# Six modulation products and the branch for large counts change places around the expert loop of a two-layer transformer

## The chip, the cores and the metric

The kernel runs on one core of one Trainium2 chip. The metric is the device time of one execution in microseconds (us), the median of several runs. A profile is one execution recorded by the hardware. The engines have short names in it: PE is TensorE's matrix multiplications and PEld its weight loads, DVE is VectorE, ACT is ScalarE, POOL is GpSimd, SP is SyncE, which only issues transfers here. A "q" behind a name means the engine's sequencer or its queue of transfers.

## The reference

Two layers work on 256 latent and 256 context tokens of 1024 features. Each layer derives six modulation vectors from a condition, mixes the tokens, and sends them through a mixture of experts (top 2 of 16). Cut to that:

```
mod   = silu(c)     @ w_ada[l] + b_ada[l]      # 6 * 1024: sh1, sc1, g1, sh2, sc2, g2
mod_c = silu(c_ctx) @ w_ada[l] + b_ada[l]
u = layer_norm(h) * (1 + sc1) + sh1
m = mixer(u)            # layer 0: window attention beside a gated recurrence; layer 1: gated linear attention, FFT
h = layer_norm_affine(alpha * h + g1 * m)
u = layer_norm(h) * (1 + sc2) + sh2
probs = softmax(u @ w_router);  two experts per token, weights w
y = sum_e gates[e] * ((silu(u @ w1[e]) * (u @ w3[e])) @ w2[e])
h = layer_norm_affine(alpha * h + g2 * y)
```

## The kernel before

The program is written with a tile framework: a scheduler orders each engine's instructions by program order and readiness, and sets the semaphores. An `If` block is a unit for it; on every engine that takes part it becomes a register load, a compare and a branch, and, where the block is skipped, events that make up for its semaphores.

**Modulation products.** The 6144 columns of `w_ada` are done in twelve products per layer, j = 0 to 11, of 512 columns. `ada_load` brings 2 MB in two loads on SP's queue into tiles "w" of the pool `wp` (three buffers). `ada_part` (L248) does eight fp32 matmuls with a 32-column stationary tile in four column groups. `ada_col` (L260) turns the result into columns: a ScalarE copy, four small matmuls (L265) and a VectorE addition. `ada_row` (L271) makes rows of it: bias on VectorE, then a broadcast matmul (L281) and a ScalarE copy (L282) for each of two destinations. j = 10 and 11 of layer 0 are the vector g2, which scales the expert output; j = 0 to 3 of layer 1 are the shift and scale that layer 1 uses first.

**Layer 0's mixer** (`mixer0`, L631) does four products at its start. The others come from a generator `fill0` (L656): one step of it is taken ahead of each of twelve weight slices of the input projections, and the remaining steps between the first steps of the recurrence (`hgrn`) and ahead of the attention. The projections are fp32r matmuls in three passes (L372).

**Router** (L499). It ranks the tokens of each expert and writes, by a matmul of one-hot matrices (L597 to L599), a list of token rows: tile `io`, with 64 rows for each of 8 units per expert. The counts go to `cni`.

**Experts of layer 0** (`moe0`, L1492). Token rows `u_d` lie in HBM. For each of 16 experts POOL gathers 64 rows, and 64 more if the count asks for it (`gathers`, L1568), by indirect transfers; TensorE transposes them (L1548), multiplies with the gate and up weights (L1478) and the down weights (L1485); ScalarE and VectorE copy the result out (L1559), and POOL scatters it to `y_d` (L1538). A third unit has its own gather. Weights come by SP's queue in tiles of 1 MB through a ring of 14 slots (`Ring`, `load_more`, L1448): nine of a pool `wx`, two of "m", three of `wp`. An expert's loads wait until a slot's last user is done. More than three units per expert are handled by `large()` (L1642), a block that stands behind the loop and is skipped when no expert has so many.

**Layer 1's mixer** (`mixer1`, L1083) loads the expert output back (`y_load`, L1119, four transfers on SP's queue), weighs the two rows of a token (L1130, L1131), scales by g2 (L1133), and normalises twice (`block`) before TensorE transposes the tokens (L1148). Two such blocks, b = 2 and 3, run interleaved, and the first weight slice of layer 1 is loaded and split into two fp32r parts (`cols_w`, L1099; ScalarE L353, VectorE L355).

## Time and profile before

| | us |
|---|---|
| median of 3 runs | 1477.45 |
| lowest and highest | 1475.44, 1483.96 |
| the profiled execution | 1482.15 |
| its span in the profile | 1480.1 |
| TensorE busy in the span | 1243.6 (84%) |
| VectorE, ScalarE, POOL busy | 603.8, 353.3, 101.0 |
| mean granted TensorE clock | 0.914 of full speed |
| HBM traffic | 303 MB read, 211 GB/s over the span |

How to read it: the busy share is a mean over stages. The stages of layer 0 are the projections (to 256 us), recurrence and attention (to 430), output projection and router (to 517), experts (525 to 848). Layer 1's mixer follows from there to about 1157, and its experts to 1460. What an edit is worth depends on the stage: on who is full there, and on what the others wait for. The clock is a share of 2.4 GHz; 0.50 is 1.2 GHz.

### The profile page before, as it was taken

The numbers are of one execution on the slowest core, as the hardware profiler recorded it, in microseconds if no ns is written. First come the engines' busy times: TensorE is split into PE (matmuls) and PEld (weight loads), VectorE is DVE, ScalarE is ACT, GpSimd is POOL, SyncE is SP. The second block draws the span as 40 slices with busy tenths as digits, with TensorE's granted clock in tenths as the row PEclk, the third lists the DMA queues.
The fourth block names the chain that finished last, engine by engine and source line by source line (L and its number), as shares of the span: only waits on it lengthen the run. The fifth ranks groups of instructions, "written<-read, shape, count | busy, mean of one in ns | idle before, by whom it ended". The sixth has DMA issues, their size and how long they took to land. (4 is left out here: it accounts for less than half of the span.)

```text
span 1480.1 us, 19008 instructions
## 1 busy us (share of the span) xinstructions
PE 1243.6 (84%) x7269; PEld 746.9 (50%) x7269; DVE 603.8 (41%) x1408; ACT 353.3 (24%) x691; POOL 101.0 (7%) x134
## 2 busy tenths in 40 slices
PE   4899999988879479999999806999977788988883
PEld 2677888455659433333333305888537443434331
DVE  5332422575857811212212148736558232222123
ACT  2333223354543110111111113442222110101001
POOL 1000000110011120211100000000010000000000
PEclk9899999897969689999999956999998899999896
DMA  8465574610012599999978052322284799988631
GB/s 296 154 231 182 185 242 173 200 29 1 1 30 86 208 328 379 362 361 380 357 280 313 14 165 82 116 64 90 86 307 144 294 394 393 383 320 324 238 134 59
DMA packets 152225, 310.32 MB, mean 210 GB/s; under 512 B 7596, under 2 KB 39660, under 8 KB 152088
## 3 DMA queue, kind: packets, MB, share of 16 engines
q1 hardware_dynamic: 146320, 296.44, 56.9%
q0 software_dynamic: 4608, 8.59, 2.0%
q10 hardware_dynamic: 1160, 3.48, 0.6%
q8 instruction: 84, 1.38, 0.4%
q14 instruction: 53, 0.43, 0.1%
HBM read 303.24 MB, written 9.44 MB: 211 GB/s over the span
## 5 line engine op out<-in xcount | busy, mean ns | idle before, releaser
L372 PE MATMUL mm<-wh,uT 128*128 128x256 f32 (+2 forms) x960 | 193.6, 297 | 7.8 <-ACT uT L353 4.8
L372 PEld LDWEIGHTS mm<-wh,uT 128*128 128x128 f32 x960 | 158.9, 198 | 21.0 <-issue 8.2
L372 PE MATMUL mm<-wl,uT 128*128 128x256 f32 (+2 forms) x480 | 141.6, 296 | 4.2 <-DVE wl L355 4.0
L1478 PE MATMUL mm<-wx,xT 128*64 128x512 f32 x504 | 143.3, 600 | 1.6 <-PEq L1619 0.8
L372 PEld LDWEIGHTS mm<-wl,uT 128*128 128x128 f32 x480 | 94.9, 198 | 6.0 <-DVE wl L355 5.4
L355 DVE TENSOR_TENSOR wl<-w,wh 128x2048 fp32r<-128x2048 f32 (+3 forms) x33 | 53.8, 1646 | 70.6 <-ACT wh L353 52.9
L1478 PEld LDWEIGHTS mm<-wx,xT 128*64 128x64 f32 x504 | 44.5, 137 | 66.6 <-issue 64.8
L1463 DVE TENSOR_TENSOR hs<-hs,mm 64x512 f32<-64x512 f32 x32 | 22.1, 691 | 127.7 <-ACT hs L1462 81.6
L254 PE MATMUL mm<-w,sT 128*32 128x512 f32 x384 | 61.7, 646 | 10.0 <-DMA w<-in_w_ada_dram 10.0
L372 PE MATMUL mm<-uT,wh 128*128 128x512 f32 (+1 forms) x208 | 59.9, 375 | 4.9 <-ACT wh L353 4.9
L1478 PE MATMUL ac<-wx,xT 128*64 128x512 f32 x216 | 60.3, 595 | 3.7 <-PEq L1865 2.1
L353 ACT CAST wh<-w 128x2048 fp32r<-128x2048 f32 (+3 forms) x33 | 45.8, 1388 | 67.2 <-DMA w<-in_w_in_even_dram 53.0
L372 PE MATMUL mm<-wo,mx 128*128 128x256 f32 x384 | 51.5, 292 | 6.3 <-ACT wo L353 3.5
L1478 PE MATMUL tr<-wx,xT 128*64 128x512 f32 x200 | 51.9, 620 | 5.1 <-PEq L1865 2.1
L1485 PE MATMUL mm<-wx,hT 128*64 128x512 f32 x192 | 54.1, 597 | 1.7 <-PEq L1634 1.0
L1462 ACT ACTIVATE hs<-mm 64x512 f32<-64x512 f32 x32 | 18.9, 590 | 147.2 <-PE mm L1478 94.4
L372 PEld LDWEIGHTS mm<-wo,mx 128*128 128x128 f32 x384 | 48.6, 197 | 7.1 <-ACT wo L353 3.8
L1478 PE MATMUL mm<-w,xT 128*64 128x512 f32 x120 | 47.0, 596 | 0.3 <-PEq L1621 0.2
L372 PEld LDWEIGHTS mm<-uT,wh 128*128 128x128 f32 (+1 forms) x208 | 37.0, 188 | 14.3 <-ACT wh L353 5.2
L1559 DVE COPY ys<-mm 64x512 f32<-64x512 f32 x22 | 15.3, 693 | 67.6 <-ACT ys L1559 64.4
L1478 PE MATMUL ac<-w,xT 128*64 128x512 f32 x88 | 41.5, 626 | 1.4 <-DMA wx<-in_w_expert_up_dram 0.7
L1148 PE MATMUL tr<-cst,yk 128*128 128x128 f32 x32 | 5.6, 334 | 43.2 <-ACT yk L1141 43.2
(472 smaller groups left out, 2162.6 us busy)
## 6 DMA issues: line engine op xcount, KB each, us to landing
w<-in_w_ada_dram SPq DMA_DIRECT2D x48, 1024.0 KB, 5.4
wx<-in_w_expert_up_dram SPq DMA_DIRECT2D x45, 1024.0 KB, 8.5
wx<-in_w_expert_gate_dram SPq DMA_DIRECT2D x42, 1024.0 KB, 7.9
wx<-in_w_expert_down_dram SPq DMA_DIRECT2D x42, 1024.0 KB, 8.0
w<-in_w_in_even_dram SPq DMA_DIRECT2D x13, 1024.0 KB, 10.1
w<-in_w_expert_down_dram SPq DMA_DIRECT2D x13, 1024.0 KB, 7.6
w<-in_w_expert_gate_dram SPq DMA_DIRECT2D x12, 1024.0 KB, 8.8
w<-in_w_expert_up_dram SPq DMA_DIRECT2D x12, 1024.0 KB
```

What stands on the lines that cost most here:

```text
L254: nc.tensor.matmul(ps[32 * g:32 * g + 32, :], sT[:, k, :], ws[k // 4][:, k % 4, :], start=k < 4, stop=k >= 4, skip_group_check=True, tile_ ...
L353: nc.scalar.copy(hi, src)
L355: nc.vector.tensor_tensor(lo, src, hi.bitcast(FP), op=OP.subtract)
L372: nc.tensor.matmul(ps, lhs(i, k), rhs(j, k), start=(k == 0 and n == 0), stop=(k == nk - 1 and n == 2))
L1148: nc.tensor.transpose(ps[:, k * 128:(k + 1) * 128], y[:, kk_ * 128:(kk_ + 1) * 128], ident)
L1462: nc.scalar.activation(hs, hp[0:64, :], AF.Silu)
L1463: nc.vector.tensor_tensor(hs, hs, hp[64:128, :], op=OP.mult)
L1478: nc.tensor.matmul(hp[i * 64:i * 64 + 64, :], xT(k), ws[2 * i + k // 4][:, k % 4, :], start=k == 0, stop=k == 7, skip_group_check=True, ti ...
L1485: nc.tensor.matmul(yp[n * 64:n * 64 + 64, :], hT[:, k, :], ws[4 + k // 2][:, k % 2, n * 512:(n + 1) * 512], start=k == 0, stop=k == 3, ski ...
L1559: (nc.vector.tensor_copy if n else nc.scalar.copy)(ys[:, ns], yp[rs_, :])
```

## The change

The products j = 10, 11 of layer 0 and j = 0 to 3 of layer 1 leave `fill0` and stand behind the last expert. Their weights are loaded through the expert ring, and the first weight slice of layer 1 (`pre`) through `wp`. `large()` stands ahead of the first expert, behind the first two gathers, and takes the slots that are free then. The index list `io` has 128 rows, so that a gather or scatter moves up to 128 rows in one transfer, without a second one and its branch; the one-hot tiles are fp32 instead of fp32r for that. The row loads of b = 2 and 3 go out on POOL's queue. The splits of `pre` stand ahead of the blocks b = 2 and 3, whose VectorE and ScalarE instructions are held in program order. In the ring the three slots of `wp` now come ahead of the two of "m".

```diff
@@ modulation products
+    def ada_load(l, j, ring=None):
         src = w_ada[l][:, j * 512:(j + 1) * 512]
-        return [load_w(src[q * 512:(q + 1) * 512, :], 4, 512) for q in range(2)], (l, j)
+        ws = []
+        for q in range(2):
+            w = ring.tile([128, 4, 512]) if ring else wp.tile([128, 4, 512], FP, name="w", tag="w")
+            nc.sync.dma_start(w, src[q * 512:(q + 1) * 512, :].rearrange("(k p) n -> p k n", p=128))
+            ws.append(w)
+        return ws, (l, j)
...
+    def ada_row(l, j, dsts, add1=0.0, col=False, ld=None, bz_=None):
+        ld = ld or ada_load(l, j)
+        if bz_ is None:
+            bz_ = bz
+            nc.gpsimd.dma_start(bz[0:2, :], b_ada[l:l + 1, j * 512:(j + 1) * 512].to_broadcast([2, 512]))
...
@@ router
-                self.io = cp.tile([64, 2, 16 * NU], I32, name="io")
+                self.io = cp.tile([128, 2, 8 * NU], I32, name="io")
...
-            R = self.p.tile([128, 2, 64], FP if self.l else FR, name="rR", bufs=1)
-            Cm = self.p.tile([128, 2, 16, NU], FP if self.l else FR, name="rCm", bufs=1)
+            R = self.p.tile([128, 2, 64], FP, name="rR", bufs=1)
+            Cm = self.p.tile([128, 2, 16, NU], FP, name="rCm", bufs=1)
...
-            for i in range(2):
-                nc.tensor.matmul(self.tps[0:64, 0:16 * NU], R[:, i], Cm[:, i].rearrange("p e j -> p (e j)"),
-                                 start=n == 0 and i == 0, stop=last and i == 1, skip_group_check=True)
+            for o in range(2):
+                for i in range(2):
+                    nc.tensor.matmul(self.tps[o * 64:o * 64 + 64, 0:8 * NU], R[:, i],
+                                     Cm[:, i].rearrange("p e j -> p (e j)")[:, o::2], start=n == 0 and i == 0,
+                                     stop=last and i == 1, skip_group_check=True, tile_position=(0, o * 64))
...
@@ fill0
-            for j, t, add1 in ((4, g1, 0.0), (5, g1, 0.0), (6, sh2, 0.0), (7, sh2, 0.0), (8, sc2, 1.0), (9, sc2, 1.0),
-                               (10, g2, 0.0), (11, g2, 0.0)):
+            for j, t, add1 in ((4, g1, 0.0), (5, g1, 0.0), (6, sh2, 0.0), (7, sh2, 0.0), (8, sc2, 1.0), (9, sc2, 1.0)):
...
-            for j in (2, 3, 0, 1, 6, 7, 8, 9):
+            for j in (6, 7, 8, 9):
...
@@ mixer1
-                    nc.sync.dma_start(yk[:, k, :], y_d[k * 512 + b * 128:k * 512 + (b + 1) * 128, :])
+                    (nc.gpsimd if b > 1 else nc.sync).dma_start(yk[:, k, :],
+                                                                y_d[k * 512 + b * 128:k * 512 + (b + 1) * 128, :])
...
+            wt = cols_w(1568, 256, pre)
             for i in range(2):
                 nc.sync.dma_start(lnr[i], (ln_g, ln_b)[i][0, 1:2, :].to_broadcast([128, D]))
+            start = len(nc.cur_bb.bb.instructions)
             for _ in blocks(2, 3, 1):
                 pass
+            in_order(start, (mybir.EngineType.DVE, mybir.EngineType.Activation))
...
@@ Ring
+        @contextmanager
+        def others(self, n):
+            kept, self.W, self.loads, self.slots, self.n = (self.W, self.loads, self.slots, self.n), {}, [], [self.slots[(self.n + i) % len(self.slots)]
+                                                              for i in range(len(self.slots) - n)], 0
+            yield
+            self.W, self.loads, self.slots, self.n = kept
...
@@ moe0
+        bzs = [xp_.tile([128, 512], FP, name=f"bz{i}") for i in range(2)]
+        for i, t in enumerate(bzs):
+            nc.vector.memset(t, 0.0)
+            nc.scalar.dma_start(t[0:2, :], b_ada[0:1, (10 + i) * 512:(11 + i) * 512].to_broadcast([2, 512]))
...
             def gathers(n):
-                x, e = xg[n % 3], SEQ[n]
-                c = e * NU
-                first = gather(x[0:64, :], io[:, 0, c:c + 1])
-                firsts.append(first)
-                with tc.If(count(e, POOL) > 2):
-                    later(gather(x[64:128, :], io[:, 0, c + 1:c + 2]))
-                return first
+                e = SEQ[n]
+                return gather(xg[n % 3], io[:, 0, e * NP:e * NP + 1])
...
             def scatters(e, ys):
-                c = e * NU
-                scatter(ys[0:64, :], io[:, 1, c:c + 1])
-                n = count(e, POOL)
-                with tc.If(n > 2):
-                    scatter(ys[64:128, :], io[:, 1, c + 1:c + 2])
-                    with tc.If(n > 4):
-                        scatter(yo[0:64, :], io[:, 1, c + 2:c + 3])
+                scatter(ys, io[:, 1, e * NP:e * NP + 1])
+                with tc.If(count(e, POOL) > 4):
+                    scatter(yo[0:64, :], io[0:64, 1, e * NP + 1:e * NP + 2])
...
-            load_more(2 + NW, [gathers(n) for n in range(2)][0])
+            f = [gathers(n) for n in range(2)][0]
+            with ring.others(nx):
+                ring.slots.append(lambda sh, dt: yst)
+                large()
+            load_more(2 + NW, f)
             gather3(0)
...
-            large()
-        return y_d
+            g2 = rp.tile([128, 2, D], FP, name="g2", tag="g2")
+            lds = [ada_load(l, j, ring) for l, j in ((0, 10), (0, 11), (1, 2), (1, 0), (1, 3), (1, 1))]
+            pre = [load_w(w_in_odd[0][q * 512:(q + 1) * 512, 1568:1824], 4, 256) for q in range(2)]
+            for ld, bz_ in zip(lds, bzs):
+                for _ in ada_row(*ld[1], [(("rowc", "rowx")[r], g2[:, r]) for r in range(2)], ld=ld, bz_=bz_):
+                    pass
+            for ld in lds[2:]:
+                ada_col(*ld[1], ld)
+        return y_d, [g2[:, 0], g2[:, 1]], pre
```

## Rows read from the trace of the kernel before

**Rows 1.** Stretches: length, each engine's busy us, TensorE's clock, DMA share, GB/s.
```profile
core 0: us, PE busy (x) PEld busy (x) DVE busy (x) ACT busy (x) POOL busy (x), PEclk, DMA share, GB/s
75.00:256.00 181.00, 179.99 (x1243) 146.12 (x1242) 50.53 (x67) 49.19 (x60) 5.14 (x10) 1.00 0.61 205
256.00:296.00 40.00, 35.60 (x253) 18.84 (x253) 21.94 (x51) 14.25 (x33) 6.46 (x12) 0.87 0.60 185
330.00:360.00 30.00, 25.95 (x107) 15.58 (x108) 18.09 (x54) 12.54 (x39) 1.95 (x4) 0.72 0.01 1
256.00:430.00 174.00, 148.92 (x1026) 91.59 (x1026) 110.64 (x307) 74.88 (x213) 16.56 (x32) 0.86 0.16 49
525.00:725.00 200.00, 191.76 (x856) 72.45 (x858) 41.23 (x60) 29.41 (x49) 29.82 (x32) 0.99 1.04 362
825.00:848.00 23.00, 21.83 (x99) 7.94 (x95) 2.77 (x4) 1.76 (x3) 0.89 (x1) 1.00 0.04 8
848.00:891.00 43.00, 0.01 (x1) 0.00 (x0) 22.70 (x51) 8.74 (x9) 3.42 (x4) 0.53 0.46 143
856.00:858.00 2.00, 0.00 (x0) 0.00 (x0) 0.00 (x0) 0.00 (x0) 0.00 (x0) 0.50 0.02 4
```

**Rows 2.** Timeline of TensorE (start, length, line, tiles, count): one product's runs.
```profile
22.56 1.05 PE L265 MATMUL tr<-cst,adas 128*128 128x2 f32 x8
...
82.15 1.88 PE L281 MATMUL mm<-adas,cst 128*128 128x512 f32 x4
...
84.39 1.92 PE L254 MATMUL mm<-w,sT 128*32 128x512 f32 x16
```

**Rows 3.** The stretch 256 to 296 us, L254 alone, then L265 alone.
```profile
256.00:296.00 40.00, 14.19 (x64) 1.97 (x64) 0.87 0.60 185
...
256.00:296.00 40.00, 3.48 (x29) 3.53 (x29) 0.87 0.60 185
```

**Rows 4.** Waits, 256 to 296 us: who for whom, us, times, longest.
```profile
ACT adas L262 <- PE mm L254: 18.3, 4, 13.3
```

**Rows 5.** Timelines of TensorE, POOL and SP around the first expert; layer 1's router.
```profile
515.77 0.47 PE L599 MATMUL ac<-rCm,rR 128*64 128x128 f32 x2 [1.89 <-DVE rCm L586]
525.04 1.94 PE L1548 MATMUL tr<-cst,xg 128*128 128x128 f32 x8 [8.80 <-DMA xg<-u_d,io]
...
517.70 1.18 POOL L1533 DMA_INDIRECT xg<-u_d,io  x1 [20.09 <-DVE pw L561]
...
518.03 0.37 SPq L1448 DMA_DIRECT2D wx<-in_w_expert_down_dram  x1
524.92 0.37 SPq L1448 DMA_DIRECT2D wm<-in_w_expert_down_dram  x1
...
1146.10 1.92 PE L592 MATMUL ac<-rCm,rR 128*64 128x16 f32 x32 [6.92 <-DVE rCm L586]
```

**Rows 6.** The branch of `large`, L1644: ns min/median/max, first and last start.
```profile
L1644 SPq EVENT_SEMAPHORE  x7: 17/17/17, 812.8 to 813.3; - x7
...
L1644 SPq TENSOR_LOAD <-cni x1: 485/485/485, 806.6 to 806.6; - x1
...
L1644 PEldq COMPARE_BRANCH  x1: 3707/3707/3707, 845.2 to 845.2; - x1
...
L1644 POOLq INC_SWDGE_SEM  x1: 1433/1433/1433, 858.8 to 858.8; - x1
```

**Rows 7.** Timeline of all engines behind the last expert.
```profile
850.40 0.89 POOL L1538 DMA_INDIRECT y_d<-ys,io  x1 [8.05 <-DVE ys L1559]
853.95 0.89 POOL L1538 DMA_INDIRECT y_d<-ys,io  x1 [2.66 <-DMA y_d<-ys,io]
860.56 0.36 SPq L1174 DMA_DIRECT2D lnr<-in_ln_g_dram  x1
...
861.80 2.09 SPq L1122 DMA_DIRECT2D yk<-y_d  x4
...
868.13 1.15 ACT L1130 ACTIVATE yk<-yk,pw 128x1024 f32<-128x1024 f32 x1 [18.86 <-DMA yk<-y_d]
```

**Rows 8.** Timeline of VectorE in the chain before the first transposes.
```profile
876.68 1.17 DVE L355 TENSOR_TENSOR wl<-w,wh 128x1024 fp32r<-128x1024 f32 x1
```

More of the change, by code (lines that the diff above doesn't have):

```diff
@@ L1 @@
-from contextlib import ExitStack
+from contextlib import ExitStack, contextmanager
 import numpy as np
@@ L1079, in mixer0, with mixer1 @@
             second(*a)
-        return h, rh, hc, [g2[:, 0], g2[:, 1]], u_d, rt
-    def mixer1(s0, sr, h, rh, hc, y_d, pw, g2s, ring):
+        return h, rh, hc, u_d, rt
+    def mixer1(s0, sr, h, rh, hc, y_d, pw, g2s, pre, ring):
         win = w_in_odd[0]
@@ L1498, in moe0 @@
         ring.slots += [lambda sh, dt: wx.tile(sh, dt, name="wx", tag="w", bufs=nx)] * nx
+        ring.slots += [lambda sh, dt: wp.tile(sh, dt, name="w", tag="w")] * NW
         ring.slots += [lambda sh, dt: rp.tile(sh, dt, name="wm", tag="m", bufs=2)] * 2
-        ring.slots += [lambda sh, dt: wp.tile(sh, dt, name="w", tag="w")] * NW
         W, load_more = ring.W, ring.load_more
@@ L1509, in moe0 @@
         hs2 = [yo[64:128, i * 512:(i + 1) * 512] for i in range(2)]
-        yss = [xp_.tile([128, D], FP, name=f"ys{i}") for i in range(2)]
+        yst = xp_.tile([128, 2, D], FP, name="ys")
+        yss = [yst[:, 0], yst[:, 1]]
         dc = xp_.tile([64, 2, 1], I32, name="dc")
+        bzs = [xp_.tile([128, 512], FP, name=f"bz{i}") for i in range(2)]
+        for i, t in enumerate(bzs):
+            nc.vector.memset(t, 0.0)
+            nc.scalar.dma_start(t[0:2, :], b_ada[0:1, (10 + i) * 512:(11 + i) * 512].to_broadcast([2, 512]))
         for t in xg + [xo_, yo] + yss:
@@ L1559, in rows_out @@
                     (nc.vector.tensor_copy if n else nc.scalar.copy)(ys[:, ns], yp[rs_, :])
-            firsts = []
-            def later(ins):
-                tc.add_manual_dep(ins.ins, firsts[-1].ins.name,
-                                  mybir.DependencyInfo(mybir.DependencyClass.NoSync, mybir.DependencyReason.DATA),
-                                  reason="the first rows come first")
-            def gathers(n):
-                x, e = xg[n % 3], SEQ[n]
-                c = e * NU
-                first = gather(x[0:64, :], io[:, 0, c:c + 1])
-                firsts.append(first)
-                with tc.If(count(e, POOL) > 2):
-                    later(gather(x[64:128, :], io[:, 0, c + 1:c + 2]))
-                return first
+            NP = NU // 2
+            def gathers(n):
+                e = SEQ[n]
+                return gather(xg[n % 3], io[:, 0, e * NP:e * NP + 1])
             def gather3(n):
@@ L1581, in gather3 @@
                 with tc.If(count(e, POOL) > 4):
-                    later(gather(xo[n % 2], io[:, 0, e * NU + 2:e * NU + 3]))
+                    gather(xo[n % 2], io[0:64, 0, e * NP + 1:e * NP + 2])
             def scatters(e, ys):
-                c = e * NU
-                scatter(ys[0:64, :], io[:, 1, c:c + 1])
-                n = count(e, POOL)
-                with tc.If(n > 2):
-                    scatter(ys[64:128, :], io[:, 1, c + 1:c + 2])
-                    with tc.If(n > 4):
-                        scatter(yo[0:64, :], io[:, 1, c + 2:c + 3])
+                scatter(ys, io[:, 1, e * NP:e * NP + 1])
+                with tc.If(count(e, POOL) > 4):
+                    scatter(yo[0:64, :], io[0:64, 1, e * NP + 1:e * NP + 2])
             def unit_up(m, ws):
@@ L1647, in large, with unit @@
                         with tc.If(nv > 3):
-                            ring.todo.extend((e, i, q) for i in range(3) for q in range(2))
+                            ring.todo[:0] = [(e, i, q) for i in range(3) for q in range(2)]
                             load_more(6)
-                            ws = W.pop(e)
-                            with tc.For_i(3, nv, 1) as jv:
-                                nc.vector.tensor_copy(dc, io[:, :, bass.ds(jv + e * NU, 1)])
+                            ws = ring.W.pop(e)
+                            def unit(o, col):
+                                nc.vector.tensor_copy(dc, io[o * 64:o * 64 + 64, :, col])
                                 gather(xo[0], dc[:, 0])
@@ L1656, in large @@
                                 scatter(yo[0:64, :], dc[:, 1])
-            nus = {}
-            load_more(2 + NW, [gathers(n) for n in range(2)][0])
+                            unit(1, slice(e * NP + 1, e * NP + 2))
+                            with tc.If(nv > 4):
+                                with tc.For_i(2, NP, 1) as jv:
+                                    for o in range(2):
+                                        unit(o, bass.ds(jv + e * NP, 1))
+            nus = {}
+            f = [gathers(n) for n in range(2)][0]
[3 more added lines that the diff above has]
+            load_more(2 + NW, f)
             gather3(0)
@@ L1912, in hybrid_dit_kernel @@
         ring = Ring(1)
-        g2, g1, rt, uh, ul = mixer1(s0, sr, h, rh, hc, y_d, rt.pw, g2, ring)
+        g2, g1, rt, uh, ul = mixer1(s0, sr, h, rh, hc, y_d, rt.pw, g2, pre, ring)
     with ExitStack() as s0:
```

19 lines of the change are left out of this document (7 added, 12 removed).

## The prediction

> **What bounds the kernel now.** I read the stretch view first: where is TensorE full, and where is it empty? From 75 to 256 us, the projections of layer 0, it is busy 179.99 of 181 us at full clock. From 256 to 430 us, recurrence and attention, it is busy 148.92 of 174 us at a mean clock of 0.86. In the expert loop of layer 0 it is busy 191.76 of the first 200 us. And from 848 to 891 us, between the last expert and layer 1, it does 0.01 us [rows 1]. So time is won where TensorE work leaves a full stretch and goes into that hole. In the hole runs a chain: the last expert's rows to HBM, back again, then VectorE's two normalisations [rows 7, 8].
>
> **Part 1: two row products leave the projections.** `fill0` is called twelve times there. Before, that gave the eight row products and four column products; after, six and four. A row product is 16 instructions of L254, 1.92 us, and two broadcasts, four instructions of L281, 1.88 us [rows 2]. That is 3.8 us each; since a run's last instruction lies over the start of the next I take 3.5, so 7.0 us off a full engine (upper end 7.6). The loads and VectorE's addition lie beside TensorE's work and give nothing.
>
> **Part 2: four column products leave the attention stretch.** From 256 to 296 us L254 is busy 14.19 us and L265 3.48 us, together 17.7 of TensorE's 35.6 us [rows 1, 3]. In these 40 us ScalarE waits 18.3 us for L254 [rows 4]. Without the products the attention's matmuls can come earlier. If all is passed on, 17.7 us come back; if the recurrence's own way through ScalarE and VectorE is as long as the stretch, none. VectorE is busy 21.94 of these 40 us and 110.64 of the 174 [rows 1], so it can take work earlier, though not without waits: I take 12, two thirds.
>
> **Part 3: the router's last step.** The index matmul becomes four in fp32 on 64 columns instead of two in fp32r on 128, which take 0.47 us. The nearest row is layer 1's fp32 form, 32 instructions in 1.92 us for 16 columns [rows 5], so eight in 0.48. If each pair took 0.47 us it would be 1.9. I take +0.5, near the row of the same form, with ends 0 and +1.4. The index operations behind it keep their number.
>
> **Part 4: the branch for large counts, in front.** The counts do not change and the branch stays untaken, so what moves is each engine's register load and jump. At its old place TensorE's compare-and-branch takes 3.7 us, and SP needs 6.7 us from the load at 806.6 to its last semaphore event at 813.3 [rows 6]. In front the first gather's flight covers them: TensorE's last router matmul starts at 515.77 us and its next work at 525.04. POOL issues the first two gathers ahead of the branch, and the third expert's gather is wanted two experts later. On SP the tenth expert load stands behind the branch. Its ninth goes out at 518.03 us; 0.4 + 6.7 us later it is 525.1, against 524.92 now, where it waits anyway [rows 5]: +0.2. The gather of 128 rows costs POOL little more than the 1.18 us of 64, since the absent rows carry no data: +0.3, upper end +1.2. I take +1.0 with what I don't see; ends 0 and +5, if TensorE's jump is scheduled ahead of the router's last matmul instead of behind it.
>
> The Trainium skill (Advanced Engine Details and Errata, Control Flow Timing) gives a compare-and-branch as about 0.108 us; TensorE's row of 3.7 us disagrees [rows 6]. By the page the branch would cost nothing at either place and part 4 would be 0.2 us lower.
>
> In the expert loop POOL loses one branch and often a second indirect transfer for each expert. TensorE keeps its own branches and is the bound: 0, ends -2 and +2.
>
> **Part 5: the products in the hole.** Their twelve loads go into ring slots that the last experts free, ahead of the hole, where the bus moves 8 GB/s from 825 to 848 us. They cost nothing there; if that cover failed, 12 MB at 362 GB/s would be 33 us [rows 1]. On TensorE, right behind 848.0 us, stand six times 1.92, two times 1.88 and four times 1.05 us (L265 [rows 2]) = 19.5 us, about 18.5 with the overlaps: until 866.5.
> Before, the path there is: scatter 850.40, second scatter 853.95 (when the first has landed), SP freed 860.56, row loads 861.80, first multiplication 868.13 us [rows 7]. The bus is silent from 856 us on [rows 1], and POOL's branch ends its semaphore work at 858.8 + 1.4 = 860.2 us [rows 6]: the branch, not the scatter, holds SP. After: one scatter, landed 3.9 us behind 850.40; two row loads on POOL at 0.5 us (SP's four in 2.09) to 1.2 (a gather [rows 5]); 6.3 us to the multiplication as now [rows 7]: 861.6 to 863. Queued ahead of it on ScalarE may be the products' copies; the last of them starts about 865. So it starts between 862 and 866; I take 865.5, 2.6 us earlier. Behind it, two weight splits of 1.2 us each that now stand in VectorE's chain [rows 8] go to the front, into the wait: 2.4 us. Together -5.0. Ends: -8.5, and +14 if TensorE did the products at 1.2 GHz (37 us, multiplication near 884.5). TensorE then idles again until its transposes, as now.
>
> The skill (DMA: Bandwidth & Descriptors, Specifications) puts the first byte at about 1 us for transfers issued from GpSimd and 0.6 us for SP's, which speaks against moving the row loads to POOL; by it the part would be -4.6. No row here shows a large plain load from POOL.
>
> **Sum.** -7.0 - 12.0 + 0.5 + 1.0 - 5.0 = -22.5 us. The profiled execution took 1482.15 us, its span 1480.1; it becomes 1459.65. It lies 4.7 us over the median of 1477.45, so I predict 1455, own range 1446 to 1463.
>
> **Rivals.**
> (a) The recurrence's own chain fills the attention stretch: part 2 gives nothing. For it: 25.1 of the 174 us without TensorE; against it: ScalarE's 18.3 us behind L254. Total -10.5: 1467.
> (b) The products run at half clock in the hole, and ScalarE's row work stands behind them. For it: the hole's clock is 0.53; against it: until 848 us it is 1.00 and TensorE would go straight on [rows 1]. Part 5 is +14, total -3.5: 1474.
> (c) Slower: without its filler TensorE falls to half clock for more of the attention stretch. 148.92 us at 0.86 are 128.1 us at full rate; less four products of 2.9 us 116.5, and 25.1 idle. At a mean clock of 0.68 the stretch lasts 196.4 instead of 174 us: +22.4 instead of -12, total +11.9, 1489. It decides against the change below a mean of 0.73. For it: 330 to 360 us, without a product, stands at 0.72 [rows 1]; against it: the mean is 0.86 although 134 of the 174 us have none.
>
> **How the numbers follow.** Forecast 0.62, (a) 0.19, (b) 0.11, (c) 0.08. A measurement can tell about 0.5%, 7.4 us. Faster: the forecast, (a), and a little of (b): 0.82. Same: (b), 0.10. Slower: 0.08. The range 1443 to 1474 reaches from part 2 at 17.7 and part 5 at -8.5 (1446, and 3 us for part 1's end and the loop) to (b).
>
> **What would show it.** Right: ten products between 75 us and the end of the projections, which end about 7 us earlier; none beside the attention; 96 instructions of L254 behind the last expert at full clock; one scatter there; the first row multiplication 14 to 18 us behind the last expert's matmul instead of 20; no weight split inside VectorE's chain. Wrong: an attention stretch as long as now, or with TensorE's clock below 0.73; an expert loop that begins over 12 us behind the router's last matmul, or in which TensorE waits for loads.

## The result and the profile after

The changed kernel takes 1492.79 us (median of 9 runs, 1487.52 to 1498.5); the kernel before took 1482.56 us in 9 runs. The ratio is 1.0072, 95% interval 1.0049 to 1.0094: about 10 us slower, where the prediction said 22 us faster. The profiled execution of after took 1493.1 us, its span is 1491.1, its clock 0.906.

Both traces were cut at the same steps of the program: the end of the last projection matmul, the last transposes of the recurrence's output, the start of the router's last run of index matmuls, the first expert's first transposes, the last expert's last matmul, the first transposes of layer 1, layer 1's first selection matmul behind its router (L1724 before, L1755 after), the last matmul. Each entry is the time from the step before; starts and ends are read from TensorE's timeline.

| stretch, us | before | after | difference | predicted |
|---|---|---|---|---|
| to the end of the projections | 255.77 | 252.03 | -3.74 | -7.0 |
| recurrence and attention | 171.34 | 171.79 | +0.45 | -12.0 |
| to the router's last matmul | 88.66 | 88.30 | -0.36 | +0.5 |
| to the first expert's transposes | 9.27 | 10.95 | +1.68 | +1.0 |
| to the end of the last expert | 322.98 | 325.13 | +2.15 | 0 |
| to layer 1's first transposes | 43.17 | 49.40 | +6.23 | -5.0 |
| to layer 1's selection | 264.89 | 272.34 | +7.45 | 0 |
| to the last matmul | 302.38 | 299.58 | -2.80 | 0 |
| sum | 1458.46 | 1469.52 | +11.06 | -22.5 |

The last row but one has nothing of the change in it; over the profiled executions below it lies between 297.3 and 302.8.

The stretches of after, in the columns of [rows 1] (PE busy, PEld, DVE, ACT, POOL, clock, DMA share, GB/s):

```profile
core 0: us, PE busy (x) PEld busy (x) DVE busy (x) ACT busy (x) POOL busy (x), PEclk, DMA share, GB/s
75.00:256.00 181.00, 173.31 (x1200) 144.51 (x1198) 52.31 (x71) 49.93 (x60) 6.19 (x11) 0.99 0.55 176
256.00:296.00 40.00, 35.32 (x199) 23.13 (x198) 26.30 (x69) 16.54 (x45) 5.37 (x11) 0.62 0.00 0
268.00:288.00 20.00, 20.00 (x104) 12.55 (x104) 10.63 (x28) 4.97 (x12) 1.95 (x4) 0.50 0.00 1
256.00:430.00 174.00, 146.59 (x926) 93.93 (x925) 109.07 (x300) 72.57 (x204) 14.16 (x28) 0.74 0.00 1
825.00:848.00 23.00, 21.83 (x100) 8.11 (x96) 2.77 (x4) 1.76 (x3) 0.98 (x1) 1.00 0.96 351
848.00:891.00 43.00, 22.37 (x138) 8.41 (x136) 16.70 (x29) 11.60 (x16) 4.74 (x7) 0.82 0.44 151
```

Three things are to be seen beside [rows 1]. Behind the projections the granted clock is 0.62 where it was 0.87, and from 268 to 288 us TensorE is busy without a gap at 0.50 and does not rise. Over the whole stretch it is busy 146.59 us instead of 148.92, though four products have left: less work, at 0.74 instead of 0.86. And the products do fill the hole (22.37 us instead of 0.01), with their loads in the quiet stretch ahead of it (351 GB/s instead of 8).

In the projections TensorE now waits for VectorE's weight splits, which it did nowhere in that stretch before (waits of TensorE, 75 to 256 us: who for whom, us, times, longest; the one line of before, then after's line):

```profile
PE tr L265 <- ACT adas L262: 0.6, 2, 0.3
...
PE mm L379 <- DVE wl L362: 4.3, 3, 2.1
```

Picked rows of the timelines of after around the first expert and behind the last (start, length, engine, line, tiles, count, idle time before and its releaser):

```profile
523.07 1.94 PE L1573 MATMUL tr<-cst,xg 128*128 128x128 f32 x8 [10.25 <-DMA xg<-u_d,io]
524.23 1.28 ACT L1574 ACT_TABLE_LOAD   x1 [19.35 <-PE tr L1573]
526.16 10.23 PE L1498 MATMUL mm<-wx,xT 128*64 128x512 f32 x32 [1.15 <-ACTq L1630]
...
848.13 1.92 PE L259 MATMUL mm<-wm,sT 128*32 128x512 f32 x16
850.59 0.97 POOL L1563 DMA_INDIRECT y_d<-ys,io  x1 [7.96 <-DVE ys L1584]
853.06 1.92 PE L259 MATMUL mm<-wx,sT 128*32 128x512 f32 x16
855.77 2.20 POOL L1130 DMA_DIRECT2D yk<-y_d  x4 [4.21 <-DMA y_d<-ys,io]
862.47 1.15 ACT L1139 ACTIVATE yk<-yk,pw 128x1024 f32<-128x1024 f32 x1 [8.70 <-DMA yk<-y_d]
863.85 1.28 DVE L1140 SCALAR_TENSOR_TENSOR yk<-yk,pw 128x1024 f32<-128x1024 f32 x1 [12.82 <-ACT yk L1139]
865.05 0.68 DVE L283 TENSOR_TENSOR adas<-mm,bz 128x512 f32<-128x512 f32 x1
865.79 3.78 PE L288 MATMUL mm<-adas,cst 128*128 128x512 f32 x4 [10.80 <-DVE adas L283]
868.53 1.23 DVE L1142 TENSOR_TENSOR yk<-yk,g 128x1024 f32<-128x1024 f32 x1 [2.80 <-ACT g L289]
...
874.33 0.17 DVE L273 TENSOR_TENSOR cols<-tr,bcol 128x8 f32<-128x8 f32 x1 [0.92 <-PE tr L270]
876.36 0.16 DVE L315 SCALAR_TENSOR_TENSOR rs<-rt,rs 128x1 f32<-128x1 f32 x1
877.94 0.17 DVE L273 TENSOR_TENSOR cols<-tr,bcol 128x8 f32<-128x8 f32 x1 [1.42 <-PE tr L270]
881.61 0.17 DVE L273 TENSOR_TENSOR cols<-tr,bcol 128x8 f32<-128x8 f32 x1 [3.50 <-PE tr L270]
885.27 0.17 DVE L273 TENSOR_TENSOR cols<-tr,bcol 128x8 f32<-128x8 f32 x1 [3.50 <-PE tr L270]
885.45 2.36 DVE L362 TENSOR_TENSOR wl<-w,wh 128x1024 fp32r<-128x1024 f32 x2
887.73 1.28 DVE L410 SCALAR_TENSOR_TENSOR hx<-hx,mv,lnr 128x1024 f32<-128x1024 f32 x1
896.11 0.16 DVE L1149 SCALAR_TENSOR_TENSOR nb<-mv,rs 128x1 f32<-128x1 f32 x1
897.60 1.97 PE L1157 MATMUL tr<-cst,yk 128*128 128x128 f32 x8 [12.36 <-ACT yk L1150]
...
912.16 0.15 DVE L1149 SCALAR_TENSOR_TENSOR nb<-mv,rs 128x1 f32<-128x1 f32 x1
913.64 1.11 PE L1157 MATMUL tr<-cst,yk 128*128 128x128 f32 x4 [14.08 <-ACT yk L1150]
```

The row multiplication (L1139) starts 14.3 us behind the last expert (848.20), where it was 20.1 [rows 7]: the scatter and the row loads did more than was predicted. But the chain from it to the first transposes grew from 23.1 to 35.1 us. The rows tell why. The second row product's addition (L283, 865.05) stands on VectorE behind the first L1140, which waits for the row loads; until then TensorE stands still for 10.8 us with its four column products behind. The product comes late for its own use too: the scaling by g2 (L1142) waits 2.80 us for it. And between 876.36 and 887.73 VectorE, in the middle of the first block's normalisation, waits in turn for three column products (1.42, 3.50, 3.50 us) and then does the weight splits. With the 0.92 us ahead of the first column addition VectorE's waits for the products add up to 12.1 us, as much as the chain grew by. Then the second block (L1149 at 912.16, transposes at 913.64) comes 16 us behind the first; before it was 9.6.

### The profile page after: what moved, and what is told of

Its sections match the earlier page's. It is cut to its first block, busy times and chain, and to the rows that moved or that the text cites. A ratio compares the mean times of both kernels' runs of the same rounds, so it can differ in the third digit from the quotient of the medians.

```text
span 1491.1 us, 18934 instructions
## 1 busy us (share of the span) xinstructions
PE 1255.1 (84%) x7293; PEld 759.2 (51%) x7293; DVE 606.5 (41%) x1410; ACT 355.3 (24%) x692; POOL 93.2 (6%) x124
## 3 DMA queue, kind: packets, MB, share of 16 engines
q0 software_dynamic: 6208, 10.69, 2.0%
## 5 line engine op out<-in xcount | busy, mean ns | idle before, releaser
L379 PE MATMUL mm<-wh,uT 128*128 128x256 f32 (+2 forms) x960 | 189.6, 293 | 3.1 <-ACT wh L360 1.9
L379 PEld LDWEIGHTS mm<-wh,uT 128*128 128x128 f32 x960 | 155.8, 195 | 14.5 <-issue 8.2
L362 DVE TENSOR_TENSOR wl<-w,wh 128x2048 fp32r<-128x2048 f32 (+3 forms) x33 | 53.8, 1649 | 69.6 <-ACT wh L360 47.7
L259 PE MATMUL mm<-w,sT 128*32 128x512 f32 x296 | 43.8, 627 | 8.6 <-DVE sT L218 7.1
L1498 PE MATMUL ac<-w,xT 128*64 128x512 f32 x104 | 44.6, 617 | 1.5 <-PEq L1896 0.8
L1498 PE MATMUL mm<-w,xT 128*64 128x512 f32 x120 | 43.1, 595 | 0.5 <-PEq L1630 0.5
L379 PE MATMUL mm<-uT,wl 128*128 128x512 f32 (+1 forms) x104 | 39.3, 381 | 1.5 <-DVE wl L362 1.5
```

What stands on the lines that cost most here:

```text
L259: nc.tensor.matmul(ps[32 * g:32 * g + 32, :], sT[:, k, :], ws[k // 4][:, k % 4, :], start=k < 4, stop=k >= 4, skip_group_check=True, tile_ ...
L362: nc.vector.tensor_tensor(lo, src, hi.bitcast(FP), op=OP.subtract)
L379: nc.tensor.matmul(ps, lhs(i, k), rhs(j, k), start=(k == 0 and n == 0), stop=(k == nk - 1 and n == 2))
L1498: nc.tensor.matmul(hp[i * 64:i * 64 + 64, :], xT(k), ws[2 * i + k // 4][:, k % 4, :], start=k == 0, stop=k == 7, skip_group_check=True, ti ...
```

## The experiments

The theories: **Q**, the order on VectorE's queue costs the boundary and layer 1; **K**, TensorE's clock ate what the products gave in the attention stretch; **B**, the branch in front costs ahead of and in the first expert. Each run is told with its time (median) and its ratio to the kernel before with the 95% interval. The table cuts the profiled execution of each as above ("early" is recurrence and attention, "gather" to the first expert's transposes, "loop" the experts of layer 0, "hole" to layer 1's first transposes, "2nd" from these to the second block's, "mixer" from the last expert to layer 1's selection).

| | projections end | early | gather | loop | hole | 2nd | mixer |
|---|---|---|---|---|---|---|---|
| before | 255.77 | 171.34 | 9.27 | 322.98 | 43.17 | 9.63 | 308.06 |
| after | 252.03 | 171.79 | 10.95 | 325.13 | 49.40 | 16.04 | 321.74 |
| hold_products | 254.66 | 171.92 | 10.69 | 325.23 | 44.87 | 16.04 | 313.67 |
| blocks_not_held | 254.04 | 168.00 | 10.61 | 324.59 | 48.98 | 9.50 | 314.36 |
| cols_back | 258.33 | 174.79 | 10.63 | 325.50 | 37.10 | 16.04 | 305.08 |
| filler_4 | 252.99 | 163.90 | 10.87 | 324.86 | 49.69 | 16.04 | 321.55 |
| branch_back | 254.85 | 166.47 | 10.18 | 324.54 | 62.44 | 16.04 | 330.96 |
| filler_1 | 252.48 | 168.28 | 10.96 | 325.30 | 49.58 | 16.04 | 321.95 |
| rows_held | 253.65 | 167.40 | 10.95 | 326.38 | 40.62 | 9.51 | 305.71 |
| rows_held_filler | 255.88 | 167.36 | 11.05 | 325.57 | 43.28 | 9.50 | 307.30 |
| products_back | 255.62 | 171.37 | 10.89 | 324.93 | 36.27 | 16.16 | 304.45 |
| best_2 | 253.54 | 166.73 | 11.24 | 323.93 | 42.47 | 9.50 | 308.15 |
| best_4 | 254.57 | 167.75 | 10.94 | 322.66 | 40.81 | 9.50 | 303.53 |

**The products first on VectorE and ScalarE (hold_products).**

```diff
+            start = len(nc.cur_bb.bb.instructions)
             lds = [
...
-            start = len(nc.cur_bb.bb.instructions)
             for _ in blocks(2, 3, 1):
```

> Edit: the held program order on VectorE and ScalarE begins ahead of the products instead of ahead of the blocks b = 2 and 3. Theory Q (queue order): in the changed kernel the second row product's addition stood on VectorE behind the first L1140 (863.85 us), so TensorE stood 10.8 us (until 865.79), and the four column additions (874.33 to 885.27) stood inside the first block's normalisation, which cost VectorE 8.9 us from 876.4 on. With the products first on both queues TensorE does all six in one go, by 867 us, the row multiplication starts at 865 to 868 instead of 862.5, and the first transposes start 39 to 42 us behind the last expert's matmul instead of 49.5 us: 8 to 10 us earlier, total about 1483, which is level with the kernel before. The second block's transposes stay about 16 us behind the first's, since the held order of the blocks is kept. Rival W (the work itself): the products' matmuls and copies cannot lie beside the row chain at all; then the transposes come no earlier than 47 us behind the last expert and the total stays at 1490 or above. Rival E (the tail is not on the path): transposes earlier but the total unchanged.

Measured: 1485.16 us, ratio 1.0023 (1.0009 to 1.0036). TensorE's wait of 10.8 us is gone and the first transposes come 4.5 us earlier, half of what was expected. The total fell by 7.6 us all the same: in the profile, another 3.5 us came between these transposes and layer 1's selection (268.8 instead of 272.3). TensorE's timeline of this run:

```profile
850.87 1.92 PE L259 MATMUL mm<-wm,sT 128*32 128x512 f32 x16
853.91 1.95 PE L288 MATMUL mm<-adas,cst 128*128 128x512 f32 x4 [1.12 <-DVE adas L283]
...
860.45 1.93 PE L259 MATMUL mm<-wx,sT 128*32 128x512 f32 x16
863.08 1.05 PE L270 MATMUL tr<-cst,adas 128*128 128x2 f32 x8 [0.70 <-ACT adas L267]
864.06 1.92 PE L259 MATMUL mm<-wx,sT 128*32 128x512 f32 x16
...
874.03 1.05 PE L270 MATMUL tr<-cst,adas 128*128 128x2 f32 x8 [0.76 <-ACT adas L267]
```

The six products take 24.2 us (850.87 to 875.08), not 18.5: each waits 0.7 to 1.1 us for its own addition or copy before its last matmuls, and a column product comes every 3.6 us. In the held order the row multiplication stands behind all of them, 24.8 us behind the last expert. Q holds for the idle time; that the products fit beside the wait for the rows does not.

**The two blocks not held (blocks_not_held).**

```diff
-            in_order(start, (mybir.EngineType.DVE, mybir.EngineType.Activation))
```

> Edit: the blocks b = 2 and 3 are no longer held in program order on VectorE and ScalarE; nothing else. Theory Q: the held order keeps block 3's normalisation from running between block 2's small steps, and lets block 0's steps come between block 3's: its L1149 came 16.05 us behind block 2's, against 7.4 us before the change. Without it the second transposes come 8 to 11 us behind the first instead of 16.0, the first ones at about the same time (the products still stand in VectorE's queue: within 3 us of 49.5 us behind the last expert), and mixer 1 ends 5 to 8 us earlier: total 1484 to 1488. Rival S (the weights or the loads of mixer 1 set its length): the second transposes come earlier, the first router step of layer 1 does not, total 1491 to 1493.

Measured: 1485.75 us, ratio 1.0039 (1.0024 to 1.0053). The first transposes stay (48.98), the second come 9.50 us behind them instead of 16.04, and layer 1's selection 7.4 us earlier; the ratios differ by 0.33%, about 5 us. With the held order VectorE does one block's small steps without the other's between them, and block 0's come between those of block 3. Rival S falls.

The held order need not be the whole of the 7.45 us that layer 1's mixer lost. From the first transposes to the selection the seven profiled executions with it took 268.0 to 272.4 us, the six without it (the kernel before among them) 262.7 to 265.7. Four of the seven, cols_back among them, lie only 3 to 4 us over the 264.89 of before. In after and filler_1, which took longest, TensorE's clock was 0.74 for 13 us about 40 us behind the first transposes; in all the others it was 1.00 there. This stretch of after, then of cols_back, columns as above:

```profile
938.00:951.00 13.00, 10.32 (x63) 9.89 (x63) 9.07 (x25) 5.18 (x8) 0.00 (x0) 0.74 0.37 107
...
935.00:948.00 13.00, 9.59 (x77) 8.68 (x75) 11.04 (x29) 5.66 (x10) 0.00 (x0) 1.00 0.34 102
```

So the held order costs 3 to 7 us, and how much of the upper end is the clock's stays open.

**The column products back (cols_back).**

```diff
-            for j in (6, 7, 8, 9):
+            for j in (2, 3, 0, 1, 6, 7, 8, 9):
...
-            lds = [ada_load(l, j, ring) for l, j in ((0, 10), (0, 11), (1, 2), (1, 0), (1, 3), (1, 1))]
+            lds = [ada_load(l, j, ring) for l, j in ((0, 10), (0, 11))]
```

> Edit: the four column products of layer 1 go back to fill0; the two row products stay behind the last expert. fill0 then has 10 + 4 = 14 products' steps: twelve fall into the projections, two into the attention stretch. Theory K (clock): in the changed kernel TensorE fell to half clock for 256 to 288 us (granted clock 0.62 in 256 to 296 against 0.87 before), which ate what the removed products gave: the stretch from the last projection matmul to the last attention matmul took 171.8 us with no product and 171.3 with four. With two it takes 165 to 172 us at a clock of 0.75 or more in its first 40 us; the projections end 3 to 4 us later again. Rival L (length of the chain through ScalarE and VectorE): the stretch stays at 171 to 172 us whatever the clock. Boundary (theory Q): only the second row addition stands wrongly; no column additions stand in VectorE's chain: the first transposes come 36 to 41 us behind the last expert instead of 49.5. Total 1480 to 1486. If the attention stretch were shortened by every product that leaves it (the prediction's term of 3 us each), it would be 5 us shorter than with four, 166 us.

Measured: 1481.52 us, ratio 0.9989 (0.9971 to 1.0008). The boundary came as Q said (37.10). The attention stretch did not: with two products its clock was 0.87 for 40 us, as with four, but 0.59 from 330 to 360 us, and it took 174.79 us, longer than K or L expected:

```profile
256.00:296.00 40.00, 34.33 (x245) 21.10 (x244) 25.27 (x61) 16.42 (x40) 6.39 (x12) 0.87 0.43 106
...
330.00:360.00 30.00, 25.89 (x125) 17.01 (x126) 17.03 (x55) 11.99 (x40) 1.95 (x4) 0.59 0.00 1
```

**Work that nobody reads, in place of the products (filler_4, filler_1).** At the first four steps (or the first one); the generator `fl` that the edit takes out has nothing left by then:

```diff
                 for n in range(4):
-                    next(fl, None)
+                    ps = mmt()
+                    for k in range(8):
+                        g = k % 4
+                        nc.tensor.matmul(ps[32 * g:32 * g + 32, :], sT[:, k, :], cst[:, 0:512], start=k < 4,
+                                         stop=k >= 4, skip_group_check=True, tile_position=(0, 32 * g))
                     yield
```

> Edit: the changed kernel with four extra blocks of eight matmuls (the shape and the place of the removed column products' matmuls, moving a constant tile, their result read by nobody) at the head of the attention stretch: 4 times about 1.9 us of TensorE work at full clock, no load, copy or addition with it. Theory K (clock): the extra work holds TensorE's clock: granted clock 0.85 or more in the 40 us behind the projections (0.62 without), and although 7 to 8 us of work are added, the stretch is no longer than 171.8 us, probably 164 to 171; total 1486 to 1493. Rival L (chain of ScalarE and VectorE): clock higher, stretch the same within 1 us. Rival P (TensorE's work is what counts, the clock is not a cause): stretch longer by 7 us or more, total 1500.

Measured: 1483.95 us, ratio 1.001 (0.9996 to 1.0023), against 1.0072 without. The stretches of this run, columns as above:

```profile
256.00:296.00 40.00, 35.91 (x262) 19.65 (x263) 29.24 (x76) 17.13 (x47) 4.65 (x11) 0.94 0.00 1
256.00:430.00 174.00, 148.36 (x1028) 93.36 (x1029) 115.57 (x303) 78.45 (x213) 19.35 (x31) 0.85 0.03 7
```

64 more matmul instructions made the kernel 0.6% faster, some 9 us: the clock stayed at 0.94 and the stretch shrank to 163.90 us. That is K; P falls, and L with it, since the chain can go 8 us faster. Whether the blocks also change the order in which the scheduler places the other work was not tried apart; the clock is what speaks for K.

> Edit: as the run with four unread blocks of matmuls at the head of the attention stretch, but only the first of the four (about 1.9 us of TensorE work at full clock). With four the stretch took 163.9 us at a clock of 0.94 in the 40 us behind the projections; with none 171.8 (168.0 and 171.9 in two other runs) at 0.62. Theory K (the clock's level in the first 40 us decides): one block brings TensorE back to full clock as early as four do (granted clock 0.85 or more in 256 to 296), stretch 162 to 166 us, total 1483 to 1487. Rival D (dose): one block is too little, the clock of the first 40 us stays at 0.6 to 0.75, stretch 168 to 174 us, total 1489 to 1494.

Measured: 1488.17 us, ratio 1.0037 (1.0015 to 1.0059). The clock of the 40 us was 0.78, the stretch 168.28: between the two. One block is less than four, so the dose counts; the size is not settled, as the stretch without any block ran from 166.5 to 171.9 us. The nine executions of this one kernel point the same way: the fastest took 1480.52 us at a mean clock of 0.920 over the whole execution, the slowest 1493.16 at 0.907.

**The branch behind the loop again (branch_back).**

```diff
-            with ring.others(nx):
-                ring.slots.append(lambda sh, dt: yst)
-                large()
             load_more(2 + NW, f)
...
+            with ring.others(nx):
+                ring.slots.append(lambda sh, dt: yst)
+                large()
             g2 = rp.tile([128, 2, D], FP, name="g2", tag="g2")
```

> Edit: the branch for large counts stands behind the expert loop again, ahead of the products; the rest as in the changed kernel. In the changed kernel the first transposes came 10.95 us behind the start of the router's last matmul (9.27 before the change), and the expert loop from there to the last expert's end took 325.1 us (323.0 before). Theory B (the branch in front costs both): ScalarE gets a second load of its function table (1.28 us ahead of its first copy of the loop) only because the branch stands there, and the queues' own branch work holds the first gather; without it 9.3 to 9.7 and 323 to 323.7 us. Rival G (the gather of 128 rows costs it): the 10.6 to 11 us stay, and only the table load goes: loop 323.5 to 324. In the boundary the branch then costs TensorE 3.7 us ahead of the first product and POOL until about 12 us behind the last expert, so the row loads go out 4 to 5 us later than now: the first transposes come 50 to 55 us behind the last expert. Total 1489 to 1494.

Measured: 1501.8 us, ratio 1.0143 (1.0102 to 1.0183), well above what was expected. Ahead of the loop 0.7 us come back (10.18; the nine profiled executions with the branch in front and the table load as it was lie at 10.61 to 11.05, mean 10.84). From the first expert's transposes to the second's it takes 11.7 us, as before the change (11.3), instead of 13.3: the table load is gone. So of the 1.6 us that these lie over the 9.27 before, 0.7 are the branch's, and 0.9 stay with the rest, that is, with what branch_back keeps. There the first gather goes out 0.3 us later behind the start of the last run of index matmuls than before the change (2.23 instead of 1.93 us), as that run takes 0.70 us instead of 0.47; and from its issue to the transposes it takes 7.96 us instead of 7.34, for which the 128 rows are the likeliest cause (G). That was not tried alone. The rest of the result is the loads (TensorE, then SP's queue, in this run):

```profile
856.18 1.93 PE L259 MATMUL mm<-wm,sT 128*32 128x512 f32 x8 [12.01 <-DMA wm<-in_w_ada_dram]
858.79 1.93 PE L259 MATMUL mm<-wm,sT 128*32 128x512 f32 x8 [0.67 <-DMA wm<-in_w_ada_dram]
...
849.72 26.54 SPq L249 DMA_DIRECT2D wx<-in_w_ada_dram  x9
```

Eleven of the twelve loads now go out behind the branch, from 848.70 us on, most likely because the skipped block uses the same ring slots. The hole is 13 us longer (62.44 instead of 49.40). The lost cover of the loads is in that, which the prediction priced at 33 us, and so is the branch's own work, since the row loads go out 14.3 us behind the last expert instead of 7.6; the two were not taken apart. Only with the branch in front did the loads lie under the last experts.

**Rows only, held up to the first block's first step (rows_held), and two unread blocks with it (rows_held_filler).** The order held from the products on (hold_products) and the column products back (cols_back), together with

```diff
-            for _ in blocks(2, 3, 1):
-                pass
+            bl = blocks(2, 3, 1)
+            next(bl)
             in_order(start, (mybir.EngineType.DVE, mybir.EngineType.Activation))
+            for _ in bl:
+                pass
```

> Edit: three in one: the four column products back in fill0; VectorE's and ScalarE's order held from the row products to the first step of the first block; the blocks b = 2 and 3 otherwise not held. Theory Q adds up: with two row products only TensorE is done 10 us behind the last expert, the row multiplication starts 14 to 15 us behind it, the first transposes come 34 to 37 us behind it (37.1 with the columns back alone, 44.9 with the order held alone, 49.4 in the changed kernel) and the second 9 to 11 us later (16.0 held). Attention stretch as with the columns back alone, 171 to 175 us. Total 1474 to 1478, ratio to the kernel before 0.995 to 0.998. Rival (the gains overlap: mixer 1 waits for weights): second transposes early, layer 1's first router step no earlier than 252 us behind the first transposes, total 1479 to 1482.

Measured: 1477.62 us, ratio 0.9968 (0.9948 to 0.9988). The time came as expected and the reason did not: from the last expert to layer 1's selection it takes 305.71 us, no less than with the columns back alone (305.08). Interleaved, the first block comes later (40.62 instead of 37.10) and the second earlier. The gains of the two edits overlap. The rival said so, but its cause is not there: none of TensorE's waits between the first transposes and the selection is for a load. What the profile of this run has over that of cols_back is its attention stretch, 167.40 us instead of 174.79; both kernels have identical code there, so this is a spread between executions and no gain of the edit, and the intervals of the two ratios overlap.

> Edit: as rows_held, and two unread blocks of matmuls (as in the run with four) behind the two column products that fall into the attention stretch. Theory K: with two products alone the clock of 296 to 330 and 330 to 360 us was 0.85 and 0.59 and the stretch 174.8 us; two more blocks of 1.9 us hold the clock up, stretch 164 to 170 us, total 1467 to 1473, ratio 0.990 to 0.995. Rival D: the blocks only add their 4 us, stretch 174 to 179 us, total 1476 to 1482.

Measured: 1477.28 us, ratio 0.9951 (0.993 to 0.9972). The stretch is 167.36, as in rows_held without the two blocks: beside two products they give nothing that shows, and cost nothing. The 174.8 us that the expectation started from was one execution of a code that took 167.4 in another.

**All products back (products_back).** As cols_back, with j = 10 and 11 in `fill0` too; the rest of the change stays.

> Edit: all six products back in fill0 as before the change (twelve steps in the projections, four products in the attention stretch); branch in front, transfers of 128 rows, row loads on POOL, early weight slice and held blocks stay as changed. It prices the move of the products alone. Attention: the four products are there again, so the stretch is a second draw of the old one: theory K (the four products hold the clock, and their own work costs about what they save) 168 to 174 us at a clock of 0.8 or more in 256 to 296 us; if the removed products had been worth 3 us each (the prediction's term) it would be 12 us longer than the changed kernel's mean of 169.5, 181. Expert loop: 10.6 to 11 us to the first transposes and 325 us, as with the branch in front. Boundary without products: the row multiplication 14 to 15 us behind the last expert, first transposes 35 to 37 us behind it, second 16.0 us later (held). Total 1480 to 1485, 8 to 12 us less than the changed kernel: the move of the products as it was made costs, not gives. Rival M (the move gives in the attention what it costs in the boundary): total 1490 to 1494.

Measured: 1482.46 us, ratio 1.0017 (1.0002 to 1.0031). Its stretch, columns as above:

```profile
256.00:296.00 40.00, 35.63 (x253) 18.80 (x254) 21.98 (x51) 14.16 (x33) 6.32 (x12) 0.87 0.59 184
```

With the same four products the attention stretch is the same to 0.03 us (171.37), clock 0.87. Without any, four profiled executions of identical code there took 171.79, 171.92, 168.00 and 166.47, mean 169.5 at 0.62. So four products, 17.7 us of TensorE's time [rows 3], were worth 1.8 us, less than the spread of the four. The move of the six as it was made costs 1.0072 less 1.0017, about 8 us; the rest of the change costs 0.2%.

**The best version (best_2, best_4).** rows_held_filler, with ScalarE's table loaded while it waits for the first gather; best_4 has an unread block at each of the four steps.

```diff
                 large()
+            tc.keep_in_program_order(nc.scalar.preload_act_table_set("silu_and_others"))
```

> Edit: rows_held_filler with ScalarE's function table for the experts loaded ahead of the first copy, in the time in which ScalarE waits for the first gather. Theory B: the load of 1.28 us leaves the first expert's path, and the second one (ahead of its first activation) with it: the time from the first expert's transposes to the second's falls from 13.7 to 14.2 us to 12 to 12.5, total 1 to 2 us under rows_held_filler: ratio to the kernel before 0.992 to 0.996. Rival: another wait of the first expert (its weights) takes its place, 13.5 us or more, no gain.

> Edit: as best_2, with an unread block of matmuls at each of the first four steps of the attention stretch instead of at the third and fourth. Theory K: with 15 us more TensorE work than the two products alone the clock of 256 to 360 us stays at 0.85 or more and the stretch lands at 163 to 168 us, as short as with the four blocks alone (163.9) although two products are there too; total equal to best_2 or up to 3 us less. Rival D (the added work counts once the clock is up): stretch 169 to 174 us, total 2 to 6 us over best_2.

Measured: 1474.98 us, ratio 0.9955 (0.9937 to 0.9972), and 1473.76 us, ratio 0.9956 (0.9939 to 0.9973). ScalarE's timeline of best_2:

```profile
508.62 1.28 ACT L1689 ACT_TABLE_LOAD   x1 [6.96 <-DVE rR L577]
521.31 0.59 ACT L1581 COPY xT<-tr 128x512 f32<-128x512 f32 x1 [11.40 <-PE tr L1580]
```

The load is off the path, and the first expert takes 12.0 and 10.6 us to the second's transposes instead of 13.7. The expectation of best_4 counts 15 us for four blocks, which at full clock are 7.7 (1.92 us each); the stretch is 167.75 us, in best_2 with two blocks 166.73, so that the number of blocks does not show beside two products. Against rows_held_filler the ratio shows no difference. Both beat the kernel before, by about 7 us.

## Why the prediction was wrong, step by step

**Part 1, -7.0, mis-sized.** The projections ended 3.7 us earlier in the profile of after, and in six profiled executions with ten products at 252.0 to 254.9 us, mean 253.5, against 255.77 before and 255.62 in products_back, which have twelve: about 2.3 us. The step that failed is "come off a full engine": the products were also what TensorE did while a weight slice was still being split; without them it waits for L362, 4.1 to 4.5 us in the six executions with ten products, 0 to 1.1 us in the seven with twelve.

**Part 2, -12.0, the step that failed most.** The prediction passed on two thirds of the removed TensorE time, 17.7 us; its own rival (c) has the same four products at 2.9 us each at full clock, 11.6 us. 0 to 2 us came (+0.45 in the profiles, -1.8 on the mean of four). It looked for the limit in VectorE's and ScalarE's chain, rival (a); filler_4 shows that this chain allows 163.9 us. The limit was the clock, and that was rival (c): its row for, 0.72 in a stretch without a product, was right, and its row against, the mean of 0.86, was misread, since the products themselves kept it there. The measured mean is 0.74. Rival (c)'s price was too high: by its formula 116.5 / 0.74 + 25.1 = 182.5 us, and 171.8 were taken: the formula has TensorE busy for 157.4 us at that clock, and it was busy for 146.59 in the 174.

**Part 3, +0.5.** The last run of index matmuls takes 0.70 us instead of 0.47, +0.23. The router's stretch as a whole changed by -0.36 us; over the profiled executions it lies between 88.0 and 89.2.

**Part 4, +1.0, mis-sized.** 1.7 us ahead of the first expert and 1.9 of the loop's 2.15 us between the first expert's transposes and the second's. The rows that the bounds rested on were the right ones, and their ends (0 to +5) hold the 3.8, but the loop's own term, 0 with ends of -2 and +2, does not hold its 2.15. What was not thought of is ScalarE: its table is loaded anew behind a branch, 1.28 us, ahead of the first copy, and TensorE waits 1.15 of it. The Trainium skill (ScalarE activation tables: per-element evaluation and per-set limits, Table sets in the compiler and the runtime) says that table loads are placed per block; the trace agrees, with two loads at the head of the loop once the branch stands ahead of it (before and in branch_back it is one), and none in the way when it is loaded early (best_2). TensorE's compare-and-branch took 6.7 us there instead of 3.7 [rows 6], and lay under the gather's flight as predicted:

```profile
L1655 PEldq COMPARE_BRANCH  x1: 6728/6728/6728, 512.7 to 512.7; - x1
```

**Part 5, -5.0, wrong in sign.** The loads were free, the row loads on POOL took 0.55 us each, at the lower bound, the bus and the branch behaved as read: the multiplication moved 5.8 us earlier, more than the 2.6 taken. Two steps failed. "About 18.5 with the overlaps" was 24.2, because a product's own copy stands between its matmuls. And "behind it, two weight splits go to the front" took VectorE's order for granted: they stayed in the chain at 885.45 us, together with the second row addition and four column additions. The prediction asked what is queued ahead of the multiplication on ScalarE and never on VectorE, where every product has an addition. Between the multiplication and the transposes 12.1 us were lost.

The Trainium skill (DMA: Bandwidth & Descriptors, Specifications) puts GpSimd's first byte 0.4 us behind SP's. From the first row load's issue to the multiplication it took 6.70 us on POOL (855.77 to 862.47) and 6.33 on SP [rows 7]: with 0.37 us, one pair of loads, the trace agrees.

**No term at all** stood for the held order of the blocks. The diff shows it, the prediction did not price it, and it cost 3 to 7 us (blocks_not_held).

Of the signs that the prediction named, ten products ahead of the attention, one scatter and a row multiplication 14 to 18 us behind the last expert (14.3) came. Projections that end 7 us earlier and a chain without a weight split in it did not come, and of its signs of being wrong the attention stretch as long as before did.

**The base.** The profiled execution was taken as 4.7 us above the median of three runs; over 28 runs the kernel before has a median of 1481.5, so that correction was wrong too.

Rival (b), products at half clock, happened in part: 3.78 and 3.02 us instead of 1.9 right behind the idle 10.8 us, full clock again from 873 us on. The slower side won by none of the rivals alone: of the 33.6 us between forecast and profile, 12.5 are the attention stretch, 18.7 the hole and layer 1's mixer, where VectorE's order does most, 3.3 the projections, 2.8 the first expert; -3.7 are elsewhere. That rival (c)'s total of 1489 us lies near the 1492.79 measured is luck: it put 22.4 us on the attention stretch, where 0.45 came, and had -5.0 for the hole.

## What to carry to other kernels

Work that seems to fill a full engine may be what keeps its clock up and hides a neighbour's latency; before taking it out, price the stretch at the lower clock that the nearest stretch without such work shows (here that price came out 10.7 us too high). When work is moved beside a latency chain, write down the order on every engine that it touches, not only on the one it loads: an in-order queue makes a small addition wait for the chain and the chain for the addition. A held order is a change of its own, with a price of its own.

## What was not expected of the hardware

TensorE ran 20 us without a gap at 0.50 of its clock (268 to 288 us), mostly on small matmuls with a few of 512 columns, and four blocks of 512-column matmuls among them held it at 0.94. What decides between the two was not settled. Without the products the length of the stretch varied by 5.5 us from execution to execution of identical code; with two it took 167.40 and 174.79 us, and with the four it was the same to 0.03 us in two.
